# Two-layer hybrid diffusion backbone: the expert input turned token-major inside the output projection

## The chip, the cores and the metric

One core of one Trainium2 chip runs the whole program. The metric is the device time of one launch in microseconds (us). The engines are TensorE (PE, with its weight loads as PEld), VectorE (DVE), ScalarE (ACT), GpSimd (POOL) and SyncE (SP, which here only issues DMAs).

## The reference, cut to what matters

256 latent and 256 context tokens of width 1024 go through two layers. Each layer has token mixers with an output projection, and then a mixture of 32 experts (4 groups of 8, the best 2 experts of the best group for each token). Only the step between the two halves matters here:

```
x = x + gt1 * y                                   # after the output projection
h = modulate(rms_norm(x, g_norm[l, 1]), sh2, sc2) # rms_norm(x, g) = x * rsqrt(mean(x*x) + eps) * g
x = x + gt2 * hier_moe(h, ...)                    # modulate(h, shift, scale) = h * (1 + scale) + shift
```

In the last layer context tokens are no longer needed, so layer 0 handles 512 tokens and layer 1 handles 256. The two token kinds have different shift and scale vectors.

## The kernel before, in words

**Layout.** The stream xT is held feature-major: 8 tiles of 128 features (partitions) by tokens (free). The experts' gather needs token-major rows: tokens on partitions, 1024 features along the free axis. Exact single-precision products on PE are made from a high and a low part (hi/lo), two fp32r tensors whose sum is the value.

**Output projection** (mixers, lines 959 to 974). Four chunks of two feature blocks each. A chunk's weights are split into hi and lo (ACT line 221, DVE line 222). Then each feature block f gets 24 matmuls (lines 333 to 335), DVE adds the gated result to xT[f] (line 971, once per 256 tokens), st.step squares it on ACT (line 272) and adds the square to a running sum on DVE or POOL (line 276), and rt.step adds the block's share of the router logits on PE (line 1052).

**Router and expert input** (moe, from line 1082). rt.finish sums the squares over features on PE (line 285), forms r = rsqrt(mean + eps) for each token (the power on POOL, line 292) and scales the logits (lines 1060, 1065). A long chain of small dependent DVE instructions (lines 1072 to 1132) finds group, experts and each token's rank in its expert, with a few small PE matmuls (line 1125) in it; the rank keys end at line 1132. The one-hot matrix S that selects tokens into expert slots is made from the keys (one_hots, line 1226).

Beside this chain stands the block that is changed, lines 1172 to 1190. st.rows spreads r over all partitions (PE line 300, ACT line 304). modulate then multiplies each xT block by r (line 322, even blocks on DVE, odd ones on POOL), and applies scale A and shift (line 327 on ACT, line 329 on DVE). PE turns every 128x128 tile (line 1187) into a PSUM bank, and split_psum makes the hi part on ACT (line 350) and the lo part on DVE (line 351): hth and htl.

**Experts.** gather (line 1231) multiplies hth and htl by S on PE (line 1237), so that every expert slot gets its token's features, and ACT copies the bank to xe (line 1241). gate_up (line 1274) multiplies xe by the fetched expert weights. All 32 experts' weights of a layer are read, 1 MB per DMA, into a few buffers; SP issues them in order, and a fetch waits until its buffer's last reader is done. Some are fetched ahead, until all buffers are full; the next one starts when gate_up has used up a buffer.

**What sets the order.** The program is traced in the order of the source, and a list scheduler with a timeline of its own (schedule_with_timeline_sim) puts the instructions on each engine's queue: source order is the priority, but a later instruction whose inputs are ready goes ahead of an earlier one that still waits. So mod_fill's chunks (lines 238 to 247, written for layer 1's modulation vectors) and the modulate block run in the gaps of the router chain. Each queue is then strictly in order on the chip. Buffers come from pools by tag: PSUM banks "mm" (4), scratch "a2" (4) and "t2" (4), slabs "mg" (2), "y" (3), "h" (4).

```
r = st.rows(rt.r)
...
modulate(l, 1, k, rt.A[:, k], hk[-1], xT[k], r, nt)
...
nc.tensor.transpose(
    q[:, o:o + 128], hk[n_][:, 256 * i + 128 * j:256 * i + 128 * j + 128], ident)
...
split_psum(hth[i][:, :, c], htl[i][:, :, c], q.rearrange("p (j c) -> p j c", j=2))
```

Of the kernel before, what the change touches and what calls it, by code (L numbers as in the profile page):

```python
# [10 lines left out]
F32 = mybir.dt.float32  # L11
# [3 lines left out]
AF = mybir.ActivationFunctionType  # L15
# [5 lines left out]
D = 1024  # L21
# [24 lines left out]
def tile_backbone(ctx: ExitStack, tc: tile.TileContext, T, out):  # L46
# [33 lines left out]
    def pmm():  # L80
        return bank("mm", 4)
# [274 lines left out]
    def mixers(l, need_ctx, xsrc, stats):  # L356
# [604 lines left out]
        for c in range(4):  # L961
            wh, wl = wsplit(w0[c], [KT, 256]) if c < len(w0) else prep(T["wout"][l, c])
            for i in range(2):
                f = 2 * c + i
                p = pmm()
                cc = slice(128 * i, 128 * i + 128)
                for k in range(KT):
                    mm3(p[:, :nq], wh[k][:, cc], wl[k][:, cc], mh[k][:, :nq], ml[k][:, :nq], k == 0, k == KT - 1)
                for v_ in range(nq // 256):
                    s = slice(256 * v_, 256 * v_ + 256)  # L970
                    nc.vector.scalar_tensor_tensor(
                        xT[f][:, s], p[:, s], modT[l][:, 16 + f, v_:v_ + 1], xT[f][:, s], op0=ALU.mult, op1=ALU.add)
                st.step(xT[f])
                rt.step(xT[f], f)
        start_fetch(l, nq)
        return st, rt

# [6 lines left out]
    def start_fetch(l, nt):  # L984
        fetched.clear()
        if nt == N:
            slot_tags[:] = ["qkv"] * 4 + ["wraw"] * 3
            fetch_up(l, 0, range(4))
        else:
            slot_tags[:] = ["qkv"] * 4 + ["mg", "y"] + ["qkv"] + ["h"] * 2 + ["wraw"] * 2 + ["mg", "wraw"] + ["whi", "wlo"] * 3  # L990
            fetch_up(l, 0)
            fetch_up(l, 1)
            fetch_down(l, 0)
# [28 lines left out]
    class Router:  # L1022
# [26 lines left out]
        def step(self, xk, k):  # L1049
            ntt = self.nt // 128  # L1050
            for t in range(ntt):
                nc.tensor.matmul(
                    self.ps[:, 36 * t:36 * t + 36], lhsT=xk[:, 128 * t:128 * t + 128], rhs=self.wA[t // 2][:, k],
                    start=(k == 0 and t == 0), stop=(k == KT - 1 and t == ntt - 1))

        def finish(self, st):
            ntt = self.nt // 128
# [24 lines left out]
    def moe(l, nt, st, rt):  # L1082
# [86 lines left out]
        nc.vector.tensor_reduce(mi[:, 0:1], mp[0:1, 0:128], axis=AX.X, op=ALU.max)  # L1169


        r = st.rows(rt.r)
        hth, htl = [], []
        for i in range(ntt // 2):
            hth.append(s8("h", [2, D], F32R))
            htl.append(s8("h", [2, D], F32R))
        for g in range(4):
            hk = []
            for k in (2 * g, 2 * g + 1):
                hk.append(t2([512]))  # L1180
                modulate(l, 1, k, rt.A[:, k], hk[-1], xT[k], r, nt)
            for i in range(ntt // 2):
                q = pmm()
                for j in range(2):
                    for n_ in range(2):
                        o = 256 * j + 128 * n_
                        nc.tensor.transpose(
                            q[:, o:o + 128], hk[n_][:, 256 * i + 128 * j:256 * i + 128 * j + 128], ident)
                c = slice(256 * g, 256 * g + 256)
                split_psum(hth[i][:, :, c], htl[i][:, :, c], q.rearrange("p (j c) -> p j c", j=2))  # L1190
        ys, Cs, ths = {}, {}, {}
        nxt = [None]

# [37 lines left out]
        def gather(S, v_, xe, k2):  # L1231

            p = pmm()
            for k in (2 * k2, 2 * k2 + 1):
                for t in range(2):
                    for part, ht in enumerate((hth, htl)):
                        nc.tensor.matmul(
                            p[:, 256 * (k % 2):256 * (k % 2) + 256],
                            lhsT=ht[v_][:, t, 128 * k:128 * k + 128], rhs=S[:, v_, t],
                            start=(t == 0 and part == 0), stop=(t == 1 and part == 1))  # L1240
            nc.scalar.copy(xe[:, 2 * k2:2 * k2 + 2], p.rearrange("p (k n) -> p k n", k=2))

        whs = tp.tile([128, 16], F32, tag="whs", name=nm("whs"), bufs=1)

# [116 lines left out]
        with tc.If(top >= 1024 + CAP):  # L1361
            over = t2([512])[:, :ntt * 32].rearrange("p (t e) -> p t e", e=32)
            nc.vector.tensor_scalar(over, key, float(1024 + CAP), None, op0=ALU.is_ge)
            nc.vector.tensor_tensor(out=dw[:, :ntt], in0=dw[:, :ntt], in1=over, op=ALU.mult)
            ec = mt[:, 512:544]
            nc.vector.tensor_copy(ec, iota32)
            hT = Slabs([s8("mg", [4, N]) for _ in range(2)], 4)
            for t in range(ntt):
                for k in range(KT):
                    q = ptr()  # L1370
                    c = slice(128 * k, 128 * k + 128)
                    nc.tensor.matmul(q[:, :128], lhsT=hth[t // 2][:, t % 2, c].bitcast(F32), rhs=ident, start=True, stop=False)
                    nc.tensor.matmul(q[:, :128], lhsT=htl[t // 2][:, t % 2, c].bitcast(F32), rhs=ident, start=False, stop=True)
                    nc.vector.tensor_copy(hT[k][:, 128 * t:128 * t + 128], q[:, :128])
            with tc.For_i(0, NQ, 1) as q4:
                for e in range(4):
                    g0, g1 = (wraw(
                        T["wgu"][l, bass.ds(q4, 1), 4 * hf:4 * hf + 4, :, e].rearrange("o k p n -> p (o k) n"), [4, 512])
                        for hf in range(2))
                    w0 = wraw(T["wdn"][l, bass.ds(q4, 1), :, :, :, e].rearrange("o c k p n -> p (o c k) n"), [4, 512])  # L1380
                    wq = small([32])
                    nc.vector.tensor_scalar(wq, ec, 0.0, 0.5, op0=ALU.is_equal, op1=ALU.mult)
                    nc.vector.tensor_scalar(ec, ec, -1.0, None, op0=ALU.add)
                    pickd = t2([512])[:, :ntt * 32].rearrange("p (t e) -> p t e", e=32)
                    nc.vector.tensor_tensor(
                        out=pickd, in0=dw[:, :ntt], in1=wq.unsqueeze(1).to_broadcast([128, ntt, 32]), op=ALU.mult)
                    wt = small([ntt])
                    nc.vector.tensor_reduce(wt, pickd, axis=AX.X, op=ALU.add)
                    aT = s8("y", [2, 512])
                    for t in range(ntt):  # L1390
                        gp = pat()
                        for k in range(KT):
                            nc.tensor.matmul(
                                gp, lhsT=hT[k][:, 128 * t:128 * t + 128], rhs=(g0, g1)[k // 4][:, k % 4],
                                start=(k == 0), stop=(k == KT - 1))
                        th = t2([512])
                        nc.scalar.activation(th[:, 0:256], gp[:, 0:256], AF.Tanh, bias=0.0, scale=0.5)
                        nc.vector.scalar_tensor_tensor(
                            th[:, 0:256], th[:, 0:256], 1.0, gp[:, 0:256], op0=ALU.add, op1=ALU.mult)
                        nc.vector.scalar_tensor_tensor(  # L1400
                            th[:, 256:512], th[:, 0:256], wt[:, t:t + 1], gp[:, 256:512], op0=ALU.mult, op1=ALU.mult)
                        q = ptr()
                        for i in range(2):
                            nc.tensor.transpose(q[:, 128 * i:128 * i + 128], th[:, 256 + 128 * i:384 + 128 * i], ident)
                        nc.scalar.copy(aT[:, :, 128 * t:128 * t + 128], q[:, 0:256].rearrange("p (a b) -> p a b", a=2))
                    for f in range(KT):
                        p = pmm()
                        for kk in range(2):
                            nc.tensor.matmul(
                                p[:, :nt], lhsT=w0[:, 2 * (f // 4) + kk, 128 * (f % 4):128 * (f % 4) + 128], rhs=aT[:, kk, :nt],  # L1410
                                start=(kk == 0), stop=(kk == 1))
                        for v_ in range(nt // 256):
                            c = slice(256 * v_, 256 * v_ + 256)
                            nc.vector.scalar_tensor_tensor(
                                xT[f][:, c], p[:, c], modT[l][:, 40 + f, v_:v_ + 1], xT[f][:, c], op0=ALU.mult, op1=ALU.add)
            if nxt[0] is not None:
                nxt[0].n = 0
                for f in range(KT):
                    nxt[0].step(xT[f])
            else:  # L1420
                for f in range(0, KT, 2):
                    emit(f)
# [112 lines left out]
```

## Time and profile before

| what | us |
|---|---|
| median of 3 runs (1631.34 to 1635.05) | 1634.6 |
| the profiled execution, its own time | 1629.37 |
| its span, first to last instruction | 1627.5 |
| PE busy in the span | 1529.6 |
| DVE busy | 788.3 |
| ACT busy | 571.8 |
| POOL busy | 183.2 |

The profile is one execution. Busy times count instructions on an engine; matmul ends are modelled, so a busy PE need not be at its peak. "xN" is a count of instructions. The granted clock (PEclk) is the share of TensorE's full clock that the chip granted. A wait is named by what ended it. Layer 0's output projection ends at 681.4 us of the span and its experts run from 714.6 us; layer 1's projection ends near 1394 us and its experts run from 1410.8 us to the end.

### The profile page before, as it was taken

To read this page: it belongs to the slowest core of one execution; us is meant where nothing else is said; L and a number is where in the kernel's file an instruction comes from. 1 tells how busy PE (TensorE), PEld (TensorE's weight loads), DVE (VectorE), ACT (ScalarE), POOL (GpSimd) and SP (SyncE) were. 2 spreads that over 40 slices of the span, in tenths; PEclk is the share of its full clock that TensorE was granted. 3 is DMA by queue.
4 is the path that set the end of the run, shared out by engine and by line. 5 is a ranking of instruction groups with operands and counts; after the bars stand their busy time and mean duration, and the time that the engine had idled before them with its cause. 6 is when DMAs were issued, how large, how long until landed. Compare 5 with 4: busy or idle time off the path is not lost. (4 is left out here: it accounts for less than half of the span.)

```text
span 1627.5 us, 26096 instructions
## 1 busy us (share of the span) xinstructions
PE 1529.6 (94%) x10725; PEld 1058.8 (65%) x10725; DVE 788.3 (48%) x1774; ACT 571.8 (35%) x1125; POOL 183.2 (11%) x162
## 2 busy tenths in 40 slices
PE   5999999999999999989999997999999999897875
PEld 3688789767767778844434435989978789632221
DVE  4637943443345425363333457378456556441222
ACT  4425642443344333131211135356355444211100
POOL 2200320100011003010000003003101112100000
PEclk9999999999999999989999998999999999898888
DMA  8552334323322154349999994542225448699998
GB/s 303 194 172 79 108 107 156 117 76 115 127 98 84 40 179 149 121 166 382 375 398 413 377 409 185 209 142 74 91 104 175 169 148 325 231 411 416 417 418 325
DMA packets 57199, 349.26 MB, mean 215 GB/s; under 512 B 6912, under 2 KB 8032, under 8 KB 20336
## 3 DMA queue, kind: packets, MB, share of 16 engines
q1 hardware_dynamic: 54720, 341.02, 54.9%
q10 hardware_dynamic: 1616, 5.24, 0.9%
q0 software_dynamic: 736, 1.24, 0.4%
q8 instruction: 88, 1.44, 0.4%
q14 instruction: 39, 0.32, 0.1%
HBM read 344.33 MB, written 3.15 MB: 213 GB/s over the span
## 5 line engine op out<-in xcount | busy, mean ns | idle before, releaser
L222 DVE TENSOR_TENSOR wlo<-wraw,whi 128x1024 fp32r<-128x1024 f32 (+1 forms) x152 | 190.6, 1254 | 169.3 <-ACT whi L221 154.2
L333 PE MATMUL mm<-h,whi 128*128 128x512 f32 (+1 forms) x656 | 226.9, 348 | 0.0
L334 PE MATMUL mm<-h,whi 128*128 128x512 f32 (+1 forms) x656 | 223.4, 342 | 0.0
L335 PE MATMUL mm<-h,wlo 128*128 128x512 f32 (+1 forms) x656 | 222.2, 342 | 0.0
L221 ACT CAST whi<-wraw 128x1024 fp32r<-128x1024 f32 (+1 forms) x152 | 155.6, 1026 | 172.3 <-PE mm L334 68.7
L333 PE MATMUL mm<-whi,h 128*128 128x256 f32 (+1 forms) x640 | 183.1, 289 | 0.0
L335 PE MATMUL mm<-whi,h 128*128 128x256 f32 (+1 forms) x640 | 182.9, 288 | 0.0
L334 PE MATMUL mm<-wlo,h 128*128 128x256 f32 (+1 forms) x640 | 182.3, 286 | 0.0
L333 PEld LDWEIGHTS mm<-h,whi 128*128 128x128 f32 x656 | 123.8, 189 | 35.5 <-issue 17.9
L335 PEld LDWEIGHTS mm<-h,wlo 128*128 128x128 f32 x656 | 123.5, 189 | 22.6 <-issue 10.1
L334 PEld LDWEIGHTS mm<-h,whi 128*128 128x128 f32 x656 | 124.2, 190 | 16.9 <-issue 5.3
L333 PEld LDWEIGHTS mm<-whi,h 128*128 128x128 f32 x640 | 121.5, 191 | 6.6 <-issue 4.0
L334 PEld LDWEIGHTS mm<-wlo,h 128*128 128x128 f32 x640 | 122.2, 191 | 1.0 <-DVE G L763 0.5
L335 PEld LDWEIGHTS mm<-whi,h 128*128 128x128 f32 x640 | 121.7, 191 | 1.5 <-issue 1.4
L1274 PE MATMUL at<-qkv,y 128*32 128x512 f32 x792 | 101.2, 606 | 8.0 <-DMA qkv<-in_wgu 8.0
L1208 DVE SCALAR_TENSOR_TENSOR qkv<-mm,c_modT,qkv 128x256 f32<-128x256 f32 x192 | 80.2, 477 | 34.6 <-PE mm L1203 34.6
L618 DVE TENSOR_REDUCE nmx<-at 128x1 f32<-128x512 f32 (+1 forms) x96 | 56.7, 598 | 54.7 <-PE at L604 53.9
L1274 PE MATMUL at<-wraw,y 128*32 128x512 f32 x552 | 73.7, 634 | 7.8 <-DMA wraw<-in_wgu 7.8
L1282 DVE SCALAR_TENSOR_TENSOR a<-a,at 128x256 f32<-128x256 f32 x24 | 10.1, 420 | 141.0 <-ACT a L1281 141.0
L536 POOL TENSOR_TENSOR s1p<-s1p,c_powm 128x8 f32<-128x8 f32 (+1 forms) x24 | 43.3, 1806 | 302.4 <-DVE s1p L534 101.1
L620 ACT ACTIVATE a<-at,nmx 128x512 f32<-128x512 f32 (+1 forms) x96 | 59.3, 619 | 34.3 <-DVE nmx L618 34.1
L1281 ACT ACTIVATE a<-at 128x256 f32<-128x256 f32 x24 | 9.2, 383 | 176.4 <-PE at L1274 171.3
(373 smaller groups left out, 2579.1 us busy)
## 6 DMA issues: line engine op xcount, KB each, us to landing
qkv<-in_wgu SPq DMA_DIRECT2D x62, 1024.0 KB, 11.6
wraw<-in_win SPq DMA_DIRECT2D x56, 1024.0 KB, 4.9
wraw<-in_wgu SPq DMA_DIRECT2D x42, 1024.0 KB, 11.4
wraw<-in_wmod SPq DMA_DIRECT2D x39, 1024.0 KB, 5.0
qkv<-in_wdn SPq DMA_DIRECT2D x31, 1024.0 KB, 9.6
wraw<-in_wdn SPq DMA_DIRECT2D x19, 1024.0 KB, 10.9
h<-in_wgu SPq DMA_DIRECT2D x14, 1024.0 KB, 17.6
wraw<-in_wbr SPq DMA_DIRECT2D x24, 512.0 KB, 3.4
```

The source lines that it names most:

```text
L221: nc.scalar.copy(hv, src)
L222: nc.vector.tensor_sub(lv, src, hv.bitcast(F32))
L333: nc.tensor.matmul(out_, lhsT=lh, rhs=rh, start=first, stop=False)
L334: nc.tensor.matmul(out_, lhsT=lh, rhs=rl, start=False, stop=False)
L335: nc.tensor.matmul(out_, lhsT=ll, rhs=rh, start=False, stop=last)
L536: nc.gpsimd.tensor_tensor(out=r, in0=v, in1=powm[:, :2 * H], op=ALU.pow)
L618: nc.vector.tensor_reduce(nmx[:, hf:hf + 1], S[hf], axis=AX.X, op=ALU.max, negate=True)
L620: nc.scalar.activation(P[hf], S[hf], AF.Exp, bias=nmx[:, hf:hf + 1], scale=1.0, accum_out=sm[:, hf:hf + 1])
L1208: nc.vector.scalar_tensor_tensor(xT[f][:, c], p[:, c], modT[l][:, 40 + f, v_:v_ + 1], xT[f][:, c], op0=ALU.mult, op1=ALU.add)
L1274: nc.tensor.matmul(gps[v_][CAP * e:CAP * e + CAP], lhsT=xe[v_][:, k, s0:s0 + CAP], rhs=w[e], start=(k == 0), stop=(k == KT - 1))
L1281: nc.scalar.activation(th[:, 0:256], gp[:, 0:256], AF.Tanh, bias=0.0, scale=0.5)
L1282: nc.vector.scalar_tensor_tensor(th[:, 0:256], th[:, 0:256], 1.0, gp[:, 0:256], op0=ALU.add, op1=ALU.mult)
```

## The change

During the output projection, after each odd feature block, a new method Router.turn scales the finished pair of xT blocks by A (without r and without the shift) on DVE, turns the tiles on PE, and copies them with ACT to token-major slabs tok. In moe, r is now a number for each partition, so that hth is tok times r on ACT and htl is tok times r minus hth on DVE, in two halves of 512 features; st.rows, modulate's second use, the turn there and the split from PSUM are gone. The shift is added after the gather, by ACT when it empties the bank (two instructions of 256 columns in place of one copy of 512), and in the overflow branch, which these inputs don't enter.

```diff
                 st.step(xT[f])
                 rt.step(xT[f], f)
+                rt.turn(xT, f)
...
+        def turn(self, xT, f):
+
+            if f % 2 == 0:
+                return
+            nt = self.nt
+            if f == 1:
+                self.tok = [s8("mg" if nt == N else "y", [2, D]) for _ in range(nt // 256)]
+            xa = []
+            for k in (f - 1, f):
+                xa.append(a2([512]))
+                for v_ in range(nt // 256):
+                    c = slice(256 * v_, 256 * v_ + 256)
+                    nc.vector.tensor_scalar(xa[-1][:, c], xT[k][:, c], self.A[:, k, v_:v_ + 1], None, op0=ALU.mult)
+            for i in range(nt // 256):
+                q = pmm()
+                for j in range(2):
+                    for n_ in range(2):
+                        o = 256 * j + 128 * n_
+                        nc.tensor.transpose(
+                            q[:, o:o + 128], xa[n_][:, 256 * i + 128 * j:256 * i + 128 * j + 128], ident)
+                nc.scalar.copy(self.tok[i][:, :, 128 * (f - 1):128 * (f + 1)], q.rearrange("p (j c) -> p j c", j=2))
...
-        r = st.rows(rt.r)
...
-        for g in range(4):
-            hk = []
-            for k in (2 * g, 2 * g + 1):
-                hk.append(t2([512]))
-                modulate(l, 1, k, rt.A[:, k], hk[-1], xT[k], r, nt)
-            for i in range(ntt // 2):
-                q = pmm()
-                for j in range(2):
-                    for n_ in range(2):
-                        o = 256 * j + 128 * n_
-                        nc.tensor.transpose(
-                            q[:, o:o + 128], hk[n_][:, 256 * i + 128 * j:256 * i + 128 * j + 128], ident)
-                c = slice(256 * g, 256 * g + 256)
-                split_psum(hth[i][:, :, c], htl[i][:, :, c], q.rearrange("p (j c) -> p j c", j=2))
+        for hf in range(2):
+            c = slice(512 * hf, 512 * hf + 512)
+            for t in range(ntt):
+                i, j, r = t // 2, t % 2, rt.r[:, t:t + 1]
+                nc.scalar.activation(hth[i][:, j, c], rt.tok[i][:, j, c], AF.Copy, scale=r)
+                nc.vector.scalar_tensor_tensor(
+                    htl[i][:, j, c], rt.tok[i][:, j, c], r, hth[i][:, j, c].bitcast(F32), op0=ALU.mult, op1=ALU.subtract)
...
-            nc.scalar.copy(xe[:, 2 * k2:2 * k2 + 2], p.rearrange("p (k n) -> p k n", k=2))
+            for k in (2 * k2, 2 * k2 + 1):
+                nc.scalar.activation(
+                    xe[:, k], p[:, 256 * (k % 2):256 * (k % 2) + 256], AF.Identity, bias=modT[l][:, 24 + k, v_:v_ + 1])
...
-                    nc.vector.tensor_copy(hT[k][:, 128 * t:128 * t + 128], q[:, :128])
+                    nc.vector.tensor_scalar(
+                        hT[k][:, 128 * t:128 * t + 128], q[:, :128], modT[l][:, 24 + k, t // 2:t // 2 + 1], None, op0=ALU.add)
```

## Rows read from the trace of the kernel before

**Rows 1.** The page: PE's busy time; granted clock and DMA share in 40 slices.
```profile
PE 1529.6 (94%) x10725; PEld 1058.8 (65%) x10725; DVE 788.3 (48%) x1774; ACT 571.8 (35%) x1125; POOL 183.2 (11%) x162
...
PEclk9999999999999999989999998999999999898888
DMA  8552334323322154349999994542225448699998
```

**Rows 2.** Busy time by stretch: steady experts, layer 0 and layer 1.
```profile
core 0: us, PE busy (x) PEld busy (x) DVE busy (x) ACT busy (x) POOL busy (x), PEclk, DMA share, GB/s
804.00:834.00 30.00, 29.39 (x247) 12.71 (x236) 10.98 (x28) 6.04 (x11) 0.00 (x0) 1.00 1.01 418
1472.00:1502.00 30.00, 21.89 (x136) 7.13 (x132) 6.65 (x16) 3.10 (x6) 0.00 (x0) 0.89 1.01 416
```

**Rows 3.** The same view: both projections, then layer 0's and layer 1's transition.
```profile
660.00:670.00 10.00, 10.00 (x54) 8.51 (x53) 3.67 (x6) 1.95 (x3) 0.00 (x0) 1.00 0.17 52
1376.00:1386.00 10.00, 10.00 (x87) 10.00 (x86) 4.27 (x7) 3.95 (x6) 2.69 (x2) 1.00 0.78 305
...
692.70:709.30 16.60, 9.26 (x52) 5.75 (x44) 16.59 (x39) 9.33 (x19) 6.86 (x4) 0.68 0.36 128
709.30:714.60 5.30, 5.24 (x32) 5.16 (x32) 5.20 (x20) 1.76 (x3) 0.00 (x0) 0.72 0.01 3
...
1397.40:1406.90 9.50, 5.23 (x22) 3.47 (x23) 9.08 (x36) 3.95 (x10) 3.40 (x5) 0.55 0.39 146
1406.90:1412.50 5.60, 5.60 (x43) 4.13 (x41) 3.81 (x13) 2.77 (x5) 0.00 (x0) 0.85 0.01 3
```

**Rows 4.** Layer 0 in order of time: r, S, gather, gate_up (start, length).
```profile
687.69 1.03 POOL L292 TENSOR_TENSOR s1p<-s1p,c_powm 128x4 f32<-128x4 f32 x1 [15.96 <-DVE s1p L291]
...
708.80 1.08 DVE L1226 TENSOR_TENSOR whi<-mt,c_iotas 128x256 fp32r<-128x256 f32 x3
...
709.36 5.33 PE L1237 MATMUL mm<-whi,h 128*128 128x256 f32 x32 [1.72 <-DVE whi L1226]
...
714.62 1.92 PE L1274 MATMUL at<-qkv,y 128*32 128x512 f32 x16
```

**Rows 5.** DVE's costliest groups from 688.6 to 709.4 us, layer 0's transition.
```profile
L329 DVE TENSOR_SCALAR t<-a,smp,c_modT 128x256 f32<-128x256 f32 x8 | 4.7, 600 | 0.0
L351 DVE TENSOR_TENSOR h<-mm,h 128x512 fp32r<-128x512 f32 x7 | 4.7, 676 | 0.0
L322 DVE TENSOR_TENSOR a<-qkv,a 128x512 f32<-128x512 f32 x4 | 4.5, 1150 | 0.0
```

**Rows 6.** DVE's costliest groups from 1397.4 to 1406.95 us, layer 1's transition.
```profile
L322 DVE TENSOR_TENSOR a<-qkv,a 128x256 f32<-128x256 f32 x4 | 2.1, 552 | 0.1
L329 DVE TENSOR_SCALAR t<-a,smp,c_modT 128x256 f32<-128x256 f32 x4 | 1.6, 399 | 0.0
L351 DVE TENSOR_TENSOR h<-mm,h 128x512 fp32r<-128x512 f32 x2 | 1.4, 676 | 0.0
```

**Rows 7.** PE's weight loads in order of time: router step, four turned tiles (twice).
```profile
679.74 1.08 PEld L1052 LDWEIGHTS at<-mt,qkv 128*128 128x128 f32 x8
...
686.97 0.50 PEld L243 LDWEIGHTS mm<-c_ident,t 128*128 128x128 f32 x4
...
705.08 0.71 PEld L1187 LDWEIGHTS mm<-c_ident,t 128*128 128x128 f32 x4 [0.16 <-ACT t L327]
```

**Rows 8.** The instructions of line 1187: ns min/median/max, first and last start.
```profile
L1187 PE MATMUL mm<-c_ident,t x48: 272/421/477, 695.0 to 1406.9; 128*128 128x128 f32 x48
```

**Rows 9.** DVE groups of the whole span: nearest shapes to the new instructions.
```profile
L829 DVE SCALAR_TENSOR_TENSOR y<-y,rd 128x512 f32<-128x512 f32 x12 | 8.9, 783 | 0.0
L712 DVE TENSOR_SCALAR qkv<-qkv,shb 128x256 f32<-128x256 f32 x12 | 3.5, 348 | 0.0
```

**Rows 10.** ACT groups of the whole span: copies, and those with a pointer operand.
```profile
L1241 ACT COPY y<-mm 128x512 f32<-128x512 f32 x48 | 28.1, 586 | 94.5 <-PE mm L1237 94.3
L570 ACT ACTIVATE qkv<-mm,c_gqkT 128x512 f32<-128x512 f32 x12 | 7.9, 687 | 0.7 <-PE mm L567 0.7
L647 ACT ACTIVATE t<-mm,c_hbm 128x256 f32<-128x256 f32 x16 | 7.6, 476 | 10.2 <-PE mm L335 9.9
```

**Rows 11.** DVE in the projection: line 222 and line 971 between 636 and 715 us.
```profile
L971 DVE SCALAR_TENSOR_TENSOR qkv<-mm,c_modT,qkv 128x256 f32<-128x256 f32 x16 | 7.0, 479 | 23.1 <-PE mm L335 23.1
L222 DVE TENSOR_TENSOR wlo<-wraw,whi 128x1024 fp32r<-128x1024 f32 x5 | 6.1, 1225 | 5.0 <-ACT whi L221 5.0
```

## The prediction

> **What bounds the kernel now.** I read the page first. PE is busy for 1529.6 us, but the slices show stretches where DMA is at nine tenths and others where it is nearly idle [rows 1]. So I read the busy times stretch by stretch. In the experts of both layers DMA is at 1.01 of its share, 418 and 416 GB/s [rows 2]: there the weight stream sets the pace, and PE can only keep up. A stage that streams weights ends as early as its stream starts, so the question is what starts it. In the projections PE is busy for all of each 10 us, while DVE has 3.7 to 4.3 and ACT 2.0 to 4.0 us of work [rows 3]: an instruction added to PE there costs its full time, one on DVE or ACT costs nothing as long as PE does not wait for it.
>
> Between the two lies the transition. The DMA share falls to 0.36 and then to 0.01 [rows 3], because every buffer is full and the next fetch waits for gate_up to free one. So a microsecond taken off the way from r to gate_up comes off the total. In layer 0 r is there at 687.69 + 1.03 = 688.72; the first one-hot starts at 708.80, the gather at 709.36 after a wait for it, gate_up at 714.62 [rows 4]. From r to the gather that is 20.6 us, and DVE is busy for 16.59 of the last 16.60 [rows 3]: DVE's queue, with the router chain and the modulate block in it, is the bound. In layer 1 the same way takes 9.5 us with DVE busy for 9.08 [rows 3]. PE is busy for half of these stretches and sets nothing.
>
> **Removed from DVE.** Layer 0: lines 329, 351 and 322 hold DVE for 4.7 + 4.7 + 4.5 = 13.9 us before the gather [rows 5]. Layer 1: 2.1 + 1.6 + 1.4 = 5.1 us [rows 6]. What also goes, line 300 on PE, lines 304 and 327 on ACT, line 322 on POOL and the turn of line 1187, stood beside DVE and is worth nothing by itself.
>
> **Added to DVE in the transition.** htl takes 8 instructions in layer 0 and 4 in layer 1, each 512 wide, both tensors in SBUF, the scalar one per partition. The trace lacks this very one; bounds are 676 ns (line 351, one source in PSUM, no pointer [rows 5]) and 783 ns (line 829, same operation, shape and kind of scalar [rows 9]). I take 783, the nearer: 6.3 and 3.1 us. So layer 0's way becomes 20.6 - 13.9 + 6.3 = 13.0, a gain of 7.6 us; layer 1's gains 5.1 - 3.1 = 2.0. The hi parts lie on ACT, 8 at about 687 ns (line 570 [rows 10]) = 5.5 us, which ends well inside 13 us, and each is ready before the lo part that needs it is due.
>
> **Added to PE.** 32 turned tiles in layer 0 and 16 in layer 1, three quarters of them between the projection's matmuls. Four tiles in a row take 0.50 us of weight loads at full clock, eight router steps 1.08 [rows 7]: 0.125 us each. A lower bound is none (if PE's modelled busy time hides slack), the upper one is the 272 ns that one takes alone [rows 8]. As the projection leaves PE no gap [rows 3], I take 0.125: 24 x 0.125 = 3.0 in layer 0, 12 x 0.125 = 1.5 in layer 1. The last turn stands beside the last router steps and the sum of squares, ahead of r; its 8 and 4 tiles I count as delay of r, 1.0 and 0.5 us (at best they fill a wait, 0). Together +6.0 us.
>
> The time between two tiles in a row, 0.125 us, is under half of what one takes alone, 272 ns [rows 7, 8]: they overlap. The rule that speaks against the change is the Trainium skill's, "TensorE: Matmul & The Clock Gate", Part 4: a turned 128x128 tile took about 275 ns in one kernel's context. By that figure as a price per tile, which [rows 7] don't bear out, the 48 tiles would cost an estimated 13.2 us and the sum would turn to a loss.
>
> **Hidden.** DVE's scaling by A: 16 and 8 instructions at 348 ns (line 712 [rows 9]) = 5.6 and 2.8 us, under PE's projection, where DVE is idle for six tenths [rows 3]; uncovered they would cost that. ACT's copies to tok: 8 and 4 at 586 ns [rows 10] = 4.7 and 2.3 us, under the same cover. The gather's emptying: two instructions of 476 ns (line 647, 256 wide from PSUM with a pointer [rows 10]) for one of 586, +0.37 us for each of 48 banks, 17.6 us of ACT, which has 6 of 30 us of work or less in the experts [rows 2]. Only before the first gate_up is there no cover: +0.37 per layer, 0.7 us. No DMA is issued, removed or moved, so SP's and POOL's queues keep their order; tok borrows slabs "mg" and "y" that merged and an early wout chunk have left by then, and gives them back before the experts ask.
>
> **Waits added.** In PE's queue each turn waits for DVE's line 971 and scaling, with the next feature block's matmuls behind it. Line 1052 has the same kind of wait and is put late enough; I cost it at nothing, with the bound under rival A.
>
> **Sum:** -7.6 - 2.0 + 6.0 + 0.7 = -2.9 us. Against the profiled execution's own 1629.37 us (span 1627.5) that gives 1626.5; the median of the runs shown, 1634.6, lies 5.2 above that execution, and the same step gives **1631.7 us**. A difference under 0.3% (4.9 us) cannot be told from none.
>
> **Rivals.**
> - **B, a shorter chain.** The one-hot needs only the keys, and the first gathers only the first half of the features. If the scheduler puts half of the lo parts behind the one-hots, 4 x 0.783 = 3.1 and 2 x 0.783 = 1.6 us more go, and with the last turn filling a wait another 1.5: -9.1, some 1626 us. For it: the chain has source priority. Against: the modulate block, too, is last in the source, and its tiles were turned at 705.08, ahead of the one-hot at 708.80 [rows 7, 4].
> - **C, a colder TensorE.** With the turn gone PE stands idle ahead of the gather. The granted clock is 0.68 from 692.7 and 0.72 in the gather [rows 3], a mix of the two levels 1.2 and 2.4 GHz. All at the lower one, layer 0's gather takes 5.3 x 0.72 / 0.50 = 7.6 us, +2.3, and layer 1's, with half the matmuls, +1.2: -2.9 + 3.5 = +0.6, 1635 us. Against: the clock fell though the turned tiles ran. The Trainium skill, same page, says that idle gaps between bursts of matmuls bring the lower clock ("Why this matters for your kernels"), and that turned tiles do not count as activity (Part 4); by the first this rival holds, by the second the change takes away nothing that kept the clock up.
> - **T, dear tiles.** At 272 ns each [rows 8]: 48 x 0.147 = +7.1 more, +4.2 in all, 1639 us. Against: [rows 7].
> - **A, PE waits in the projection, slower than before.** PE's queue is in order; a turn that comes up before DVE has its input stops all matmuls behind it. In layer 0 DVE needs 2 x 0.479 + 2 x 0.348 = 1.65 us after a block's last matmul, in layer 1 half, 0.83; if a weight split (line 222, 1.225 us) stands ahead [rows 11, 9], 2.9 and 2.05. Three turns per layer inside the projection: up to 14.8 us, so 1646; at half of it 1639. From 2.9 / 6 = 0.5 us per turn on the gain is lost.
> - **The change does not do what it says:** each queue is planned anew, so distant stretches can move by some us either way. This widens every case.
>
> **Chances.** Forecast 0.40 (its own range 1628 to 1635), B 0.24, C 0.10, T 0.10, A 0.16. Faster by over 0.3% is below 1629.7: all of B and the lower third of the forecast, 0.14, together 0.38. Slower, above 1639.5: most of A (0.14) and the upper part of T (0.04), 0.18. The rest, 0.44, is no change. For 8 in 10 the range goes from 1623 (B with 676 ns per lo part and a free last turn) to 1641 (T, and A at half price).
>
> **What would show it.** Right: DVE from r to the gather falls to about 13 and 7.5 us; the projections grow by 3.0 and 1.5 us with PE still busy throughout; lines 322, 329 and 350 lack the expert input's instructions and POOL is idle in the transition; DMA's pause shortens by the same amount. Wrong: waits of PE for DVE inside the projection (A), turned tiles more than 0.2 us apart (T), a gather that takes 7 us at 0.50 (C), one-hots that still start 20 us after r, or an experts' stage that doesn't end as much earlier as it begins, which would mean the stream isn't its bound.

## The result, and the profile after

The changed kernel takes 1647.8 us (median of 4 runs, 1646.2 to 1650.1) where the kernel before took 1633.0 in the same session: a ratio of 1.0093, 95% interval 1.0071 to 1.0116. That is slower by some 15 us, outside the range, and on the side to which 0.18 was given. The profiled execution took 1648.1 us with a span of 1646.2, which is 18.7 more than the span of before.

The page's busy times, granted clock and DMA share, as in [rows 1]:

```profile
PE 1538.1 (93%) x10713; PEld 1063.5 (65%) x10713; DVE 787.7 (48%) x1778; ACT 583.7 (35%) x1171; POOL 172.6 (10%) x154
...
PEclk9999999999999999889999999999999999898898
DMA  8542334323322153159999895642234458499998
```

The page alone says little: PE is busy for 8.5 us more with 12 fewer instructions, and that is all. Matmuls that became longer while there are fewer of them point to the clock; where, the stretches say. The busy times by stretch, with the stretches that answer to [rows 2, 3] (projection of layer 0, of layer 1, then layer 0's way from r to the gather, its gather, layer 1's way from r, the steady experts):

```profile
core 0: us, PE busy (x) PEld busy (x) DVE busy (x) ACT busy (x) POOL busy (x), PEclk, DMA share, GB/s
660.00:670.00 10.00, 7.52 (x32) 5.92 (x32) 4.22 (x8) 1.68 (x2) 1.55 (x1) 0.69 0.30 107
1386.00:1396.00 10.00, 8.27 (x56) 8.15 (x56) 3.61 (x8) 3.10 (x4) 0.73 (x1) 0.83 0.76 310
700.60:718.20 17.60, 10.70 (x96) 5.53 (x94) 12.70 (x47) 7.95 (x17) 0.01 (x1) 0.78 0.74 274
718.20:723.70 5.50, 5.50 (x32) 5.38 (x32) 5.33 (x22) 2.27 (x6) 0.00 (x0) 0.69 0.21 83
1417.20:1425.00 7.80, 0.27 (x4) 0.19 (x3) 7.34 (x32) 2.98 (x6) 0.00 (x0) 0.56 0.32 114
...
804.00:834.00 30.00, 29.38 (x244) 13.18 (x236) 12.28 (x30) 5.88 (x13) 0.00 (x0) 1.00 1.02 419
```

In the projections PE was busy for 10.00 of 10 us before [rows 3]; now it has 7.52 and 8.27, and the granted clock is 0.69 and 0.83 where it was 1.00. The steady experts are what they were. Layer 0's transition in order of time, as in [rows 4] (line 1241 makes the one-hots, 1252 gathers, 1291 is gate_up; line 292's end is r; line 246 belongs to a modulation chunk):

```profile
699.58 1.03 POOL L292 TENSOR_TENSOR s1p<-s1p,c_powm 128x4 f32<-128x4 f32 x1 [15.83 <-DVE s1p L291]
...
711.38 0.17 DVE L246 TENSOR_REDUCE c_modT<-mm 128x4 f32<-128x16 f32 x1 [3.31 <-PE mm L243]
...
717.60 0.76 DVE L1241 TENSOR_TENSOR whi<-mt,c_iotas 128x256 fp32r<-128x256 f32 x2
...
718.18 5.61 PE L1252 MATMUL mm<-whi,h 128*128 128x256 f32 x32 [0.98 <-DVE whi L1241]
...
723.72 1.92 PE L1291 MATMUL at<-qkv,y 128*32 128x512 f32 x16
```

Such stamps, taken for all stages, give the whole account. A projection goes from the start of its first line 971 to that of its last; e1 is the first experiment below, the change with banks of its own for the turn.

| stage, us | before | after | e1 |
|---|---|---|---|
| layer 0: start of the projection's first line 971 | 637.3 | 638.8 | 638.2 |
| projection | 44.2 | 56.3 | 46.8 |
| its end to r | 7.2 | 5.5 | 8.0 |
| r to the gather | 20.6 | 17.6 | 11.6 |
| gather to gate_up | 5.3 | 5.5 | 5.4 |
| gate_up to layer 1's first line 971 | 659.7 | 660.3 | 661.0 |
| layer 1: projection | 19.9 | 29.9 | 21.1 |
| its end to r | 3.2 | 3.3 | 3.3 |
| r to the gather | 9.6 | 7.8 | 7.8 |
| gather to gate_up | 3.8 | 5.7 | 6.1 |
| gate_up to the end of the span | 216.7 | 215.5 | 216.3 |

The projections lost 12.1 and 10.0 us. The ways from r to the gather gained 3.1 and 1.8, and layer 1's gather gave 1.9 of that back. After each gate_up the rest takes as long as before to about a microsecond: what is late at gate_up is late at the end.

**What PE waits for.** Behind the second feature block of layer 0 (layout: start, length, engine, line, what; in brackets the idle time ahead of it and what ended it):

```profile
643.60 1.87 PE L1053 MATMUL at<-mt,qkv 128*128 128x36 f32 x16
...
643.79 0.88 DVE L971 SCALAR_TENSOR_TENSOR qkv<-mm,c_modT,qkv 128x256 f32<-128x256 f32 x2 [0.59 <-PE mm L335]
644.69 1.22 DVE L222 TENSOR_TENSOR wlo<-wraw,whi 128x1024 fp32r<-128x1024 f32 x1
...
645.41 1.62 POOL L276 TENSOR_TENSOR acc<-acc,a 128x512 f32<-128x512 f32 x1 [13.32 <-ACT a L272]
645.83 2.14 DVE L1069 TENSOR_SCALAR a<-qkv,smp 128x256 f32<-128x256 f32 x4
...
647.24 0.74 PE L1075 MATMUL mm<-c_ident,a 128*128 128x128 f32 x2 [1.77 <-DVE a L1069]
...
647.63 0.78 PE L333 MATMUL mm<-h,whi 128*128 128x512 f32 x1
...
648.20 0.63 PE L334 MATMUL mm<-h,whi 128*128 128x512 f32 x1
...
651.18 0.40 PE L334 MATMUL mm<-h,whi 128*128 128x512 f32 x1
```

Line 971, then a weight split's lo part (line 222), then the scaling (line 1069) stand one behind the other on DVE, and PE, with its router step (line 1053) done, stands still for 1.77 us until 647.24. What it then runs is odd: two turned tiles, not eight. They are the first tile of each of the turn's two banks, and behind them the next block's matmuls follow at once; the other six come some 6 us later. So those matmuls waited not for the turn's result but for its place. The turn takes its banks from the tag "mm", as the projection does; a tag's buffers are handed out in the order of the source, and the next block's banks come behind the turn's. The scheduler puts the first tiles in PE's queue to open the banks, and all of the next block stands behind them.

PE's waits in the two projections (what it waited for, us in total, times, longest; layer 0 first):

```profile
PE mm L1075 <- DVE a L1069: 3.7, 2, 1.9
PE at L1053 <- DVE qkv L971: 1.7, 3, 0.6
...
PE at L1053 <- DVE qkv L971: 2.6, 4, 0.9
PE mm L1075 <- DVE a L1069: 2.5, 2, 1.3
```

Together they are 10.5 us, against 0.2 in the kernel before. The wait for the scaling comes in the first two turns of each layer alone; in the third PE goes straight from the router step to the turned tile.

The second thing is in the last rows of the list above: line 334 takes 0.63 us at 648.20, 0.40 at 651.18, and the matmuls start 0.43 us apart instead of 0.23. The granted clock falls to 0.50, the lower level of 1.2 GHz, once PE has stopped, and stays there while PE is busy again. Behind the third turns it stays at 1.00. In windows of 2 us behind the second such stop:

```profile
664.00:666.00 2.00, 0.87 (x3) 0.79 (x4) 1.77 (x4) 0.00 (x0) 0.84 (x1) 0.50 0.10 41
666.00:668.00 2.00, 2.00 (x6) 1.55 (x5) 0.00 (x0) 0.00 (x0) 0.00 (x0) 0.50 0.03 8
668.00:670.00 2.00, 2.00 (x6) 1.52 (x6) 0.00 (x0) 0.00 (x0) 0.00 (x0) 0.50 0.00 0
670.00:672.00 2.00, 2.00 (x9) 1.64 (x8) 0.00 (x0) 0.00 (x0) 0.00 (x0) 0.84 0.00 0
```

The theory for the experiments: 22 us of loss in the projections, made of stops for the turn's banks, of the lower clock behind each stop, and of the turned tiles themselves; without the first two the change would come out near the sum that was forecast. The rival: the tiles, scalings and copies are simply too much for the projection, wherever they stand.

### The profile page after: what moved, and what is told of

Same layout as the page of the kernel before. It is cut to its first block, busy times and chain, and to the rows that moved or that the text cites. A ratio compares the mean times of both kernels' runs of the same rounds, so it can differ in the third digit from the quotient of the medians.

```text
span 1646.2 us, 26101 instructions
## 1 busy us (share of the span) xinstructions
PE 1538.1 (93%) x10713; PEld 1063.5 (65%) x10713; DVE 787.7 (48%) x1778; ACT 583.7 (35%) x1171; POOL 172.6 (10%) x154
## 5 line engine op out<-in xcount | busy, mean ns | idle before, releaser
L333 PE MATMUL mm<-h,whi 128*128 128x512 f32 (+1 forms) x656 | 230.5, 353 | 0.0
L334 PE MATMUL mm<-h,whi 128*128 128x512 f32 (+1 forms) x656 | 226.7, 346 | 0.0
L333 PEld LDWEIGHTS mm<-h,whi 128*128 128x128 f32 x656 | 126.7, 194 | 35.8 <-issue 17.9
L334 PEld LDWEIGHTS mm<-h,whi 128*128 128x128 f32 x656 | 126.6, 193 | 17.4 <-issue 5.3
L1291 PE MATMUL at<-qkv,y 128*32 128x512 f32 x792 | 106.6, 610 | 7.1 <-DMA qkv<-in_wgu 7.0
## 6 DMA issues: line engine op xcount, KB each, us to landing
qkv<-in_wgu SPq DMA_DIRECT2D x62, 1024.0 KB, 11.6
```

Of the source, the lines that this page charges most:

```text
L333: nc.tensor.matmul(out_, lhsT=lh, rhs=rh, start=first, stop=False)
L334: nc.tensor.matmul(out_, lhsT=lh, rhs=rl, start=False, stop=False)
L1291: nc.tensor.matmul(gps[v_][CAP * e:CAP * e + CAP], lhsT=xe[v_][:, k, s0:s0 + CAP], rhs=w[e], start=(k == 0), stop=(k == KT - 1))
```

## Experiments

Each is timed beside the kernel before on the same chip; ratios are to it, with 95% intervals.

**e1, banks of its own.** The turn takes its PSUM banks from two tags that the projection leaves alone. Nothing else differs from the changed kernel.

```diff
-                q = pmm()
+                q = (ptr, pao)[i]()
```

> The changed kernel, but the turn takes the PSUM banks tr and ao (unused in the projection) in place of two of the four mm banks. Theory (the order of the banks): buffers of one tag are handed out in the order of the source, so the next feature block's matmuls cannot be put on PE's queue until the first turned tile of each of the turn's banks is; with other banks those matmuls go first. Expected: PE's waits for DVE in the projection gone, granted clock 1.00 throughout, projections 3 and 1.5 us longer than in the kernel before, layer 0's transition without the stop of DVE behind the modulation chunks; 1627 to 1633 us, some 15 to 20 below the changed kernel. Rival (the volume of the turn: 48 tiles, 24 scalings, 12 copies, contention with POOL): the work is the same, so the time stays at 1644 or above.

1628.6 us (11 runs), ratio 0.9987 (0.9974 to 1.0001). The same window of the projection, the way from r to the gather in both layers, and between them layer 0's gather:

```profile
660.00:670.00 10.00, 10.00 (x56) 8.52 (x54) 4.76 (x8) 2.76 (x4) 1.03 (x1) 1.00 0.05 19
692.90:704.50 11.60, 3.35 (x40) 1.53 (x28) 11.18 (x40) 6.02 (x13) 0.04 (x1) 0.70 0.69 274
704.50:709.90 5.40, 5.35 (x32) 5.26 (x32) 5.23 (x22) 2.26 (x6) 0.00 (x0) 0.71 0.00 0
1395.30:1403.10 7.80, 0.24 (x3) 0.15 (x3) 7.30 (x32) 2.98 (x6) 0.01 (x1) 0.62 0.36 135
```

PE is busy throughout again, at full clock, with all turns, scalings and copies in the projection. This one line takes back the whole loss and 2 us more: 0.0106 x 1631 = 17 us between the two ratios. The projections are 2.6 and 1.3 us longer than before: that is the true price of 24 and 12 tiles, 0.107 and 0.105 us each. DVE is busy for 11.18 of 11.60 us from r to the gather, so it is still the bound there, with less to do. The rival falls.

**e2, the old banks, but late.** The turn keeps tag "mm" and is put in the source behind the next block's matmuls.

```diff
+                if f > 0:
+                    rt.turn(xT, f - 1)
...
-                rt.turn(xT, f)
+        rt.turn(xT, KT - 1)
```

> The changed kernel with mm banks, but each turn stands in the source behind the 24 matmuls of the next feature block; the last one behind the loop. Theory (order of the banks): three of four waits per layer go, the last turn still stands ahead of the modulation chunks' banks, so layer 0's transition stays some 4 us long: 1631 to 1638 us. Rival (volume): 1644 or above.

1631.5 us, ratio 1.0000 (0.9988 to 1.0012). The same banks cost some 2 us, and not 17, when the input is ready by the time that their place in the order comes up. By the stamps, from the projection's start to gate_up it takes 1.8 us more than e1 in layer 0 (r to the gather is 15.05 us, with the last turn in it) and 1.1 in layer 1, and another 3.0 between layer 0's gate_up and layer 1's projection, whose reason stays open.

**e3 and e4, the wait by itself.** The kernel before, with a probe behind every odd block: one scaling, one turned tile, one copy of 8 columns that nobody reads. 8 tiles in all, no other part of the change. In e3 the tile goes into a bank "mm", in e4 into "tr".

```diff
+                if f % 2:
+                    xa = a2([512])
+                    nc.vector.tensor_scalar(xa[:, :256], xT[f][:, :256], rt.A[:, f, 0:1], None, op0=ALU.mult)
+                    q = pmm()
+                    nc.tensor.transpose(q[:, :128], xa[:, :128], ident)
+                    nc.scalar.copy(small([8]), q[:, :8])
```

> The kernel before with a small probe behind the router step of each odd feature block: one scaling of 256 columns on DVE, one turned 128x128 tile into an mm bank, one copy of 8 columns on ACT; the rest as before. 8 tiles in all in place of 48. Theory (order of the banks): PE still has to wait for DVE before the next block, and the clock falls with it; 8 to 18 us slower than the kernel before. Rival (volume): a sixth of the changed kernel's loss, 0 to 3 us.

> The same probe with its tile in the bank tr. Theory (order of the banks): the next block's matmuls go ahead, and 8 tiles at 0.125 us cost 1 us: within 2 us of the kernel before. Rival (volume): the same as with the mm bank.

e3: 1650.0 us, ratio 1.0115 (1.0098 to 1.0132). e4: 1632.5, ratio 1.0011 (1.0002 to 1.0020). Eight tiles that take about 0.1 us each cost some 19 us in the one bank and 2 in the other; e3 even lies a little over what was expected. The tag is the whole difference. PE's waits in e3 are nearly those of the changed kernel, 3.7 + 1.7 us in layer 0 and 2.5 + 2.7 in layer 1; e4 has none in layer 0. Of e3, the busy times around the first stop:

```profile
643.00:645.00 2.00, 1.23 (x11) 1.11 (x10) 1.98 (x4) 1.05 (x2) 0.83 (x1) 1.00 0.97 287
645.00:647.00 2.00, 1.00 (x3) 0.90 (x4) 0.95 (x1) 0.17 (x1) 0.80 (x1) 0.61 0.56 238
647.00:649.00 2.00, 2.00 (x6) 1.52 (x6) 0.00 (x0) 0.00 (x0) 0.00 (x0) 0.54 0.00 0
```

and of e4, its whole projection:

```profile
644.00:690.00 46.00, 46.00 (x272) 38.04 (x270) 16.61 (x26) 9.91 (x17) 4.60 (x3) 1.00 0.28 95
```

**e7 and e10, the clock by itself.** The changed kernel with unused matmuls ahead of the turn in the first two turns, so that PE works through the stop: in e7 in layer 0 alone, in e10 in both layers (there 14 of 256 columns). If the lower clock is only a sign of the stop, nothing changes; if it costs by itself, the projection gets shorter although work is added.

```diff
+            if f < 4 and nt == N:
+                fill = ptr()
+                for i in range(12):
+                    nc.tensor.matmul(
+                        fill[:, :nt], lhsT=self.mh[0][:, 0:128], rhs=self.mh[0][:, :nt], start=True, stop=True)
```

> The changed kernel with 12 more matmuls of 512 columns (result unused, bank tr) in each of the first two turns of layer 0, which the scheduler puts into PE's wait for DVE. Theory (half of the loss at a turn is the wait, half the lower clock after it): the granted clock stays at 1.00 behind these two waits, and the time between line 971 of the blocks on either side falls from 11.5 and 12.7 us to about 9; some 5 us below the changed kernel, although PE has 24 matmuls more to do. Rival (the clock follows something else, or the wait alone costs the time): the clock falls to 0.50 as before, and the time stays or rises by up to 5 us.

> The changed kernel with unused matmuls ahead of the turn in the first two turns of both layers (12 of 512 columns in layer 0, 14 of 256 in layer 1). If the lower clock behind each stop is a cost of its own, layer 1's granted clock stays at 1.00 through its projection, the blocks that follow a stop's block come back from 3.5 to 2.4 us each, and the projection takes 26.5 to 28.5 us instead of 29.9; layer 0's projection takes 53.4 us again. The time is 3 to 6 us under the changed kernel, unless the wait of 4 us in which the profile shows nothing stands between the layers again; then it is 0 to 2. Rival: the fill lengthens the stops by as much as the clock gives, and layer 1's projection stays at 29.9 us.

e7: 1649.6 us, ratio 1.0122 (1.0098 to 1.0147), a miss. e10: 1644.7, ratio 1.0090 (1.0074 to 1.0105), which is the changed kernel's ratio. The clock itself did as expected, in e7:

```profile
664.00:666.00 2.00, 1.98 (x13) 1.57 (x13) 1.28 (x4) 0.00 (x0) 0.34 (x1) 1.00 0.00 0
666.00:668.00 2.00, 2.00 (x10) 1.67 (x9) 0.00 (x0) 0.00 (x0) 0.00 (x0) 1.00 0.00 0
668.00:670.00 2.00, 2.00 (x13) 1.69 (x13) 0.00 (x0) 1.07 (x2) 0.00 (x0) 1.00 0.00 0
```

Layer 0's projection takes 53.4 us in both instead of 56.3, and layer 1's 28.0 in e10 instead of 29.9. From the second block's line 971 to the third's it is 10.9 us and not 11.5, from the fourth's to the fifth's 10.4 and not 12.7. So at least 2.9 and 1.8 us are the clock's own (the fill lengthens the first stop of layer 0, whose turned tiles start 4.26 us after line 971 and not 3.45, so the clock's share there is larger), and gate_up is reached sooner (counted from the projection's start, 81.7 and 81.3 us in layer 0 instead of 84.9). One part of e10's expectation fell: the blocks behind a stop's block still take 3.6 us and not 2.4, so what lengthens them is not the clock. In e10 it is a weight split once more: line 222 (1.23 us from 1392.56) stands on DVE ahead of the next block's line 971 (972 there), which starts at 1393.70, and PE waits 0.92 us for it. Then the gain goes. From layer 0's gate_up to layer 1's first line 957 e7 takes 3.7 and e10 5.7 us longer than the changed kernel, and in this stretch each has one wait in which PE is held by nothing that the profile shows. Of e10, PE's waits from 700 to 1400 us (waited for, us in total, times, longest):

```profile
PE ao L285 <- issue: 6.0, 1, 6.0
PE ao L285 <- PEq L1384: 3.7, 1, 3.7
```

The second line stands in all kernels, the first is 3.9 us in e7, 6.0 in e10, and not there in the changed kernel. It stands between the layers, where the program branches. What it is stays open; no run was made for it.

**e8, all turns behind the loop.** Banks as in e1.

```diff
-                rt.turn(xT, f)
+        for f in range(KT):
+            rt.turn(xT, f)
```

> The kernel with own banks, with all four turns in the source behind the projection's loop. Theory (a tile costs its 0.1 us of PE wherever PE is the bound): the projections are as short as in the kernel before, and the tiles stand ahead of r or beside the chain instead, where PE idles: between 2 us faster and 3 us slower than with own banks. Rival (the turn's place decides): over 5 us away from it.

1627.5 us, ratio 0.9986 (0.9973 to 0.9999), the same as e1. The projections take 44.2 and 19.9 us as before the change, and the way from r to the gather 13.4 and 8.5 instead of 11.6 and 7.8. So it doesn't matter where the turns stand, as long as no matmul of the projection waits for them: PE pays the tiles in one place or in the other.

**e6, a plain copy after the gather.** e1, with one copy of 512 columns to empty the gather's bank; the shift is left out.

```diff
-            for k in (2 * k2, 2 * k2 + 1):
-                nc.scalar.activation(
-                    xe[:, k], p[:, 256 * (k % 2):256 * (k % 2) + 256], AF.Identity, bias=modT[l][:, 24 + k, v_:v_ + 1])
+            nc.scalar.copy(xe[:, 2 * k2:2 * k2 + 2], p.rearrange("p (k n) -> p k n", k=2))
```

> The kernel with own banks, with the gather's banks emptied by one plain copy of 512 columns as before; the shift is left out of the expert input. It tells what the two instructions with a pointer cost. Theory: they are hidden except ahead of the first gate_up: 0 to 1.5 us faster than the kernel with own banks. Rival (ACT holds back the gathers, so PE and the stream): more than 3 us faster, and layer 1's gate_up after three gathers instead of four.

1625.5 us, ratio 0.9975 (0.9963 to 0.9987), about 2 us under e1 by the two ratios, 0.0012 x 1631: between the two expectations, with intervals that overlap. In the two profiles nothing is gained ahead of a gate_up: from the projection's start it takes 72.6 us in layer 0 (e1: 71.7) and 38.2 in layer 1 (38.3). The stretch that is shorter is that of layer 0's experts, 659.0 us and not 661.0. Layer 1's gate_up still waits for 32 gather matmuls (from 1399.57 to 1405.55), so the longer emptying is not why four gathers go ahead of it.

**e5 and e9, a better version.** e5 is e1 with the second half of the features scaled late: its r is made from the first one-hots' tile, so it can't go ahead of them. e9 is e5 with all turns behind the loop, as in e8.

```diff
+        r2 = small([ntt])
+        nc.vector.scalar_tensor_tensor(
+            r2, S[:, ns - 1, 1, 0:ntt].bitcast(F32), 0.0, rt.r, op0=ALU.mult, op1=ALU.add)
+        scale_half(1, r2)
```

> The kernel with own banks, and the scaling by r of the second 512 features made to depend on the first one-hots (its r is r plus 0 times a column of S), so that it cannot go ahead of the router chain. Theory (what is left of the loss: lo parts fill the chain, and in layer 1 all four gathers, ready at once, go ahead of gate_up, 6.1 us from the gather's start to gate_up against 3.8): r to gather falls from 11.6 to about 8.5 us in layer 0 and from 7.8 to about 6.3 in layer 1, layer 1's gather to gate_up from 6.1 to about 4; 4 to 8 us below the kernel with own banks. Rival (the experts' stream is bound elsewhere, so an earlier gate_up gives nothing): within 1.5 us of it.

> Banks of their own, all turns behind the projection's loop, and the second half of the features scaled behind the first one-hots: the two edits that each came out ahead of the first, together. If they add, layer 0's r stands at 689 as with the late turns, the gather 9 to 11 us behind it, gate_up by 705 to 707, and the time is 0 to 3 us under the late half alone, 1622 to 1626 us. Rival: the copies of the late turns hold ACT's queue just when it should make the first hi parts, so the gather starts no sooner than 702 and the time stays at 1625 to 1628.

e5: 1625.4 us (12 runs), ratio 0.9971 (0.9957 to 0.9986): under the kernel before by 4.7 us, with the interval clear of 1. Layer 0 of e5, in order of time:

```profile
691.99 1.03 POOL L292 TENSOR_TENSOR s1p<-s1p,c_powm 128x4 f32<-128x4 f32 x1 [17.43 <-DVE s1p L291]
...
702.28 6.41 PE L1254 MATMUL mm<-whi,h 128*128 128x256 f32 x32 [0.95 <-DVE whi L1243]
...
707.61 0.75 DVE L1204 SCALAR_TENSOR_TENSOR h<-mg,s1p,h 128x512 fp32r<-128x512 f32 x1
708.62 2.07 DVE L1204 SCALAR_TENSOR_TENSOR h<-mg,s1p,h 128x512 fp32r<-128x512 f32 x3
...
708.62 2.78 PE L1293 MATMUL at<-qkv,y 128*32 128x512 f32 x24
```

The gather starts 9.3 us after r, 2.3 sooner than in e1, but takes 6.3 until gate_up instead of 5.4. Both gathers are 32 matmuls; the granted clock in them is 0.58 here and 0.71 in e1. That need not come from the edit: e6 has e1's instructions ahead of its gather, and there it is 0.59, and 6.2 us. The second half's lo parts (line 1204) now run from 707.61 to 710.69, one ahead of gate_up's start and three from there on. Measured against e1 the gain is some 2.6 us by ratio, with intervals that overlap, under the 4 to 8 expected and above the rival's 1.5. e9: 1625.6, ratio 0.9969 (0.9959 to 0.9980). It is 0.3 us under e5 by ratio, far inside the intervals, and the ranges of both expectations contain its time, so it does not tell them apart. The gather starts 11.0 us after r, at 701.64 (the rival had no sooner than 702), and gate_up at 708.23, where 705 to 707 was expected. As e8 gave nothing over e1, there was little to add.

## Why the prediction was wrong

**Where it failed.** The step is "Waits added": a turn waits for DVE's line 971 and scaling with the next block's matmuls behind it, "I cost it at nothing". Its comparison was line 1052, which "has the same kind of wait and is put late enough". That step can be put late because nothing that PE does next needs the bank it writes to. The turn's banks are of the tag from which the next block draws, and so it can't. The diff had it in plain sight, `q = pmm()`, and the text before had "mm" with four banks; e3 against e4 shows that this one word is worth 17 us. The wait was seen, priced under rival A, and given 0.16.

**Rival A's price was near.** It had up to 14.8 us for six stops, each with a weight split ahead. Of 22.1 us that the projections grew, e1's 2.6 + 1.3 = 3.9 are the tiles and at least 2.9 + 1.8 = 4.7 the lower clock; what remains, 13.5 or less, goes with the stops. The trace shows 10.5 of it as waits of PE; some 3 are not broken down. That 14.8 lies so near is in part luck: only four of the six turns have a weight split ahead and make PE wait for their scaling, and the scalings took longer than A had them. What A lacked was the clock. The Trainium skill says in "TensorE: Matmul & The Clock Gate" ("Why this matters for your kernels") that idle gaps between bursts of matmuls bring the lower clock; the prediction brought it up for the transition alone. The trace agrees with it in the projection: 0.50 for 3 to 6 us behind two stops of PE in layer 0, where it stood still for 1.8 and 1.9 us, and 1.00 where the stop is filled. With A's price and the clock in place of nothing the sum is -2.9 + 14.8 + 4.7 = +16.6 us; measured by ratio, +15. That this fits is luck too, since layer 0's way from r to the gather gained 3.1 us and not 7.6.

**The terms that held.** Groups of the changed kernel that answer to the durations taken [rows 9, 10], first DVE, then ACT:

```profile
L1069 DVE TENSOR_SCALAR a<-qkv,smp 128x256 f32<-128x256 f32 x24 | 9.9, 467 | 0.0
L1204 DVE SCALAR_TENSOR_TENSOR h<-mg,s1p,h 128x512 fp32r<-128x512 f32 x8 | 5.9, 749 | 0.2
...
L1257 ACT ACTIVATE y<-mm,c_modT 128x256 f32<-128x256 f32 x96 | 40.0, 471 | 88.7 <-PE mm L1252 86.3
L1203 ACT ACTIVATE h<-mg,s1p 128x512 fp32r<-128x512 f32 x8 | 5.3, 720 | 3.9 <-POOL s1p L292 3.9
```

- The lo part takes 749 ns (783 taken), the hi part 720 (687), the emptying 471 (476).
- r to the gather was to become 13.0 and 7.5 us; it is 11.6 and 7.8 where no bank is in the way (e1). In the changed kernel layer 0 has 17.6, since the wait struck a second time: the modulation chunks' banks stand behind the last turn's, their fetch goes out at 703.5 us instead of 682.6, and DVE, whose queue has line 246 ahead of the router chain, stands idle from 708.1 to 711.4 us. In e1 that wait is gone; that the banks' order makes it is read from the source and from e1, not tested by itself. "No DMA is issued, removed or moved" was thus wrong for those fetches.
- A tile costs 0.106 us (0.125 taken). The rule that was set against it, 275 ns a tile (the Trainium skill, "TensorE: Matmul & The Clock Gate", Part 4), would have made 13.2 us of 48 tiles. In e1 the 36 tiles inside the projections cost 3.9 us, and 48 at that price 5.1; so rival T falls, and with it that figure as a price per tile. The 272 ns that the prediction calls a tile's time alone are the shortest record of its line [rows 8]; no row shows a tile alone.
- The last turn was to delay r by 1.0 and 0.5 us; in e1 it is 0.8 and 0.1.
- The stream: what is gained or lost ahead of a gate_up arrives at the end, to about a microsecond, in the changed kernel and in e1, as the views of [rows 2] said. e2, e7 and e10 lose 3 to 6 us on the way.

**The terms that were too small.** The scaling takes 467 ns on average and not 348, and its cover held only where PE doesn't wait for it. The emptying was to cost 0.7 us; by e6 it is about 2, an estimate with overlapping intervals, and by the two profiles it lies in the experts, where it was called covered, and not ahead of the first gate_up. And layer 1's gain of 1.8 us ahead of the gather went in the gather: 3.8 us became 5.7. Before, PE had 24 gather matmuls ready and did gate_up's next; now hth and htl are whole when the one-hots come, and 32 go ahead of it. At the 0.16 us that one matmul of the gather took before, 32 would take an estimated 5.1 us (32 x 3.83 / 24). The granted clock shows where the rest may lie; the gather of layer 1 before, changed and in e5 (columns as above, granted clock third from the end):

```profile
1406.99:1410.82 3.83, 3.83 (x27) 3.63 (x25) 3.72 (x13) 2.09 (x4) 0.00 (x0) 0.79 0.00 0
...
1424.97:1430.67 5.70, 5.70 (x34) 5.60 (x34) 2.15 (x10) 2.33 (x6) 0.00 (x0) 0.70 0.01 3
...
1401.78:1406.96 5.18, 5.18 (x24) 4.95 (x24) 3.71 (x13) 3.01 (x6) 0.00 (x0) 0.50 0.00 0
```

In e5, where half of hth comes late, only 21 gather matmuls go ahead, and yet they take 5.2 us, at 0.50. The shares of count and clock are argued from these rows; no run parts them.

**The other rivals.** B, a late second half by the scheduler's choice, did not happen (in e1 all eight lo parts of layer 0 stand ahead of the one-hots); forced in e5 it gives 2.6 us of the 4.7 that its lo parts were priced at. C's colder gather did not come in layer 0, where the gather of the changed kernel and of e1 runs at 0.69 and 0.71 (0.72 before [rows 3]). In layer 1 it came in part: 0.70 and, in e1, 0.65 for 0.79.

## What to carry to other kernels

A new user of a shared buffer tag takes a place in the order of all its users: price it by when its input is ready against when the next user wants to start, and give it a tag of its own if it is later. In an in-order queue, an instruction costs not what it takes but what stands behind it; each of the four stops that were filled here had cost at least another 0.5 to 2.4 us in clock. A term that is "hidden" has to be tested with the wait that would uncover it, before it is set to nothing.

## What the runs showed of the hardware

A scaling of 256 columns on DVE takes 348 ns at line 712 [rows 9], but 1.35 us in e3 where it starts while POOL adds two tiles (line 276):

```profile
644.17 1.62 POOL L276 TENSOR_TENSOR acc<-acc,a 128x512 f32<-128x512 f32 x1 [13.31 <-ACT a L272]
644.59 1.35 DVE L977 TENSOR_SCALAR a<-qkv,smp 128x256 f32<-128x256 f32 x1
```

It ends 0.15 us after POOL does, at 645.94 and 645.79. The Trainium skill has this in "SBUF — State Buffer", "Who interferes with whom": the two engines share a port pair, which a scaling on DVE can take if it runs in a mode that uses both of its ports; one engine holds the pair for a whole instruction while the other is blocked. The row agrees, though it doesn't show the mode: the scaling takes the rest of POOL's instruction and some more. In the changed kernel this lengthened the first stop, four scalings in 2.14 us; in the third turn, most of which lies ahead of POOL's instruction, four take 1.13.

The other surprise is the wait of PE behind the branch between the layers, 3.9 and 6.0 us with nothing in the profile that holds it, in two kernels that differ from the changed one only by unused matmuls in the projection. The kernel before has one of 3.2 us in the same stretch, at line 399, and there the way from gate_up to the next projection is no longer than in the changed kernel (659.7 and 660.3 us); so such a wait's cost can't be read from its length alone.
